# Twenty-seven fp32 products in two halves: norm factors, norm sums and cross attention's values

## The chip, the cores and the metric

The kernel runs on one core of one Trainium2 chip. The metric is the device time of one execution in microseconds; lower is better. Before the change the median of three runs was 877.38 us (877.32 to 877.93). TensorE (PE) does the products, ScalarE (ACT) and VectorE (DVE) the elementwise work, GpSimd (POOL) a few masks and sums, and SyncE (SP) issues the transfers of the weights.

## The reference

Two transformer blocks run one after the other on 256 tokens of width 1024, all in fp32. Cut to what matters here:

```
# first block
u = rms_norm(h, g_mix) @ w_in
ya = diff_attention(...)            # 4 heads; each head's output is normed: rms_norm(o, g_subln)
yb = stick_breaking_attention(...)  # 8 heads
h = h + concat(ya, yb) @ w_out
# cross attention, 4 heads of 256 columns, over 256 memory rows
q = rms_norm(h, g_cross) @ w_xq;  k, v = split(rms_norm(mem, g_mem) @ w_xkv)
h = h + (softmax(q k^T / 16) v) @ w_xo
h = h + square(relu(rms_norm(h, g_mlp) @ w_up)) @ w_down          # MLP, 4096 wide
h = rms_norm(h, g_final)
# second block
proj = _rmsnorm(h, norm1_g) @ w_in                                 # 6308 columns
y_a, y_b = _nsa_mixer(...), _dilated_mixer(...)
x = h + (sigmoid(g_ma) * (y_a @ w_o_a) + sigmoid(g_mb) * (y_b @ w_o_b)) @ w_out
x = x + square(relu(_rmsnorm(x, norm2_g) @ w_up)) @ w_down          # MLP, 4096 wide
# rms_norm(x, g) = x * rsqrt(mean(x*x) + 1e-6) * g
```

## The kernel before

Activations are kept with the model dimension on the partitions and the 256 tokens on the free axis, in eight chunks of 128x256.

**Split products.** Every weight matrix and every activation that meets one is split into a coarse part and a rest, both of type fp32r (`wunit`, lines 240 and 243, for weights; `split1` for activations). A product is then three products of one pass each: coarse by coarse, rest by coarse, coarse by rest. `mm3` (lines 276 to 278) does it with the weights stationary and 256 token columns streaming; `gemm_n` (lines 329 to 331) with the activations stationary and the weights' columns streaming, 256 or 292 of them; `acc_add` (lines 344 to 348) as `mm3` does, in another order. `gemm_t` and `out_rows` call `mm3`: the MLPs, the queries of cross attention, the memory's keys, the gates and all output matrices are of this kind. The projections of the mixers are mostly `gemm_n`.

**Full fp32 products.** Products of small tensors are not split; they stay fp32, and each leaves two records on PE. Transposes (line 449) leave one. Among the full products are:

- `row` (line 432): per-token factors, which stand one to a partition, are put on a diagonal, and a matrix of ones spreads them over all 128 rows: one product of 128x128 by 128x256. It is called five times: for the first block's norm, for the memory's norm, for cross attention's, and twice for the second block's.
- `rstd_t` (line 441): a matrix of ones sums squares over the partitions and spreads the sums, again one product by 256 columns. It is called for each of the four heads in `da_values`, and once in each MLP, after unit 2 of 16.
- `cross_values` (line 918): probabilities, transposed, by the memory's values. For each of four heads there are two halves of the output (`j`) and two halves of the memory (`kt`): four products by 256 columns, 16 in all. All go to one PSUM bank, which `split1` then reads.

Other full products keep their shape: the scores (lines 560 to 563, 660 to 663, 894), the stick-breaking sums (578 to 580), the values of the other attentions (670 to 673, 707, 708), and the sums of `rstd_n` (line 408), whose streamed operand has one column.

**Order.** `build` writes the blocks one after the other; inside a stage a `Filler` mixes generators of projection products into the attention heads' code. The order on each engine is then settled by a planner: the kernel is built under `tile.TileContext(nc, schedule_with_timeline_sim=True)`, which lays the program out by its own estimates, and by dependences that the code adds (`after`). `row` takes such a dependence for its product (`after`). All weight transfers go out on SP's queue into six raw buffers. The PSUM pool has three banks `G`, two `Z`, two `X` and one `O`; the results of the three changed functions all use `O`.

Of the kernel before, what the change touches and what calls it, by code (L numbers as in the profile page):

```python
# [17 lines left out]
P = 128  # L18
T = 256
NT = 2  # L20
# [114 lines left out]
class Builder:  # L135
# [289 lines left out]
    def row(self, r, tag, after=None):  # L425

        ps = self.Oo()
        d = self.t([P, NT, P], "diag")
        for tt in range(NT):
            self.nc.vector.tensor_scalar(out=d[:, tt], in0=self.ident, scalar1=r[:, tt:tt + 1], scalar2=None,  # L430
                                         op0=ALU.mult)
        i = self.nc.tensor.matmul(ps[:, :T], self.ones, d.rearrange("p t q -> p (t q)"), start=True, stop=True)
        if after is not None:
            self.after(i, after)
        out = self.t([P, T], tag)
        self.row_copy = self.nc.scalar.activation(out, ps[:, :T], AF.Copy)
        return out

    def rstd_t(self, acc, n, tag):
        ps = self.Oo()  # L440
        self.nc.tensor.matmul(ps[:, :T], self.ones, acc, start=True, stop=True)
        r = self.t([P, T], tag)
        self.rsqrt(r, ps[:, :T], 1.0 / n)
        return r
# [462 lines left out]
    def cross_values(self, p, mv, h, o):  # L907
        nc, mm = self.nc, self.nc.tensor.matmul
        ps = self.X((P, 2, T))
        for kt in range(NT):  # L910
            for tt in range(NT):
                self.transpose(ps[:, kt, tt * P:(tt + 1) * P], p[:, tt, kt * P:(kt + 1) * P])
        pt = self.t([P, 2, T], "xpt")
        nc.scalar.activation(pt, ps, AF.Copy)
        po = self.Oo((P, 2, T))
        for j in range(2):
            for kt in range(NT):
                mm(po[:, j], mv[:, kt, (2 * h + j) * P:(2 * h + j + 1) * P], pt[:, kt], start=(kt == 0), stop=(kt == 1))
        self.split1(o[0][:, 2 * h:2 * h + 2], o[1][:, 2 * h:2 * h + 2], po)


# [631 lines left out]
```

## Time and profile before

| | |
|---|---|
| median of 3 runs | 877.38 us (877.32 to 877.93) |
| profiled execution | 875.89 us, of which the span from the first to the last instruction is 874.2 us |
| mean granted clock of TensorE | 0.997 |
| PE busy | 858.7 us (98%), 7099 records |
| DVE, ACT, POOL busy | 599.6, 552.6, 90.0 us |
| DMA | 144.68 MB, 166 GB/s in the mean |

The profile is of one execution. "Busy" is the time in which an engine has at least one instruction under way; products overlap in PE, so a record's duration (some 280 ns for a split product) is longer than the distance from its start to that of the next one. In the timeline, a row is a start time, a duration, and how many equal instructions in a row it stands for; the distance between the starts of two rows, divided by the number of products that begin in it, is the time that each takes from PE. A stretch is a piece of the span, given in us from its start.

### The profile page before, as it was taken

How to read it: one execution, taken by the hardware profiler on the slowest of the kernel's cores; microseconds unless marked ns; L12 is line 12 of the kernel's file. 1: busy time of each engine (PE TensorE's matmuls, PEld its weight loads, DVE VectorE, ACT ScalarE, POOL GpSimd, SP SyncE). 2: the span in 40 equal slices, each digit the busy share in tenths (PEclk: the TensorE clock that was granted, in tenths of full speed). 3: DMA queues.
4: the chain of work that ended last, by engine and by line, in shares of the span. 5: the costliest groups of instructions: out<-in, count | busy, mean ns of one | idle time of the engine just before them, and what ended most of it. 6: DMA issues, size and time to landing. Idle time of an engine off the chain costs nothing.

```text
span 874.2 us, 18293 instructions
## 1 busy us (share of the span) xinstructions
PE 858.7 (98%) x7099; PEld 824.5 (94%) x7099; DVE 599.6 (69%) x1295; ACT 552.6 (63%) x1204; POOL 90.0 (10%) x131
## 2 busy tenths in 40 slices
PE   9999999999999999999999999999988999999998
PEld 9989989999999999999998998889977999999997
DVE  7646687585698555665977786786947985555564
ACT  7769577564565555664674987877755665555551
POOL 0032200020020000000203130113410300000000
PEclk9999999999999999999999999999999999999999
DMA  9664535652466566766377454232623565556531
GB/s 312 191 198 160 167 96 150 198 185 73 146 204 196 184 187 192 239 200 196 86 254 240 121 170 121 73 97 74 220 95 94 166 216 184 187 193 192 182 134 49
DMA packets 111862, 144.68 MB, mean 166 GB/s; under 512 B 6304, under 2 KB 100128, under 8 KB 111776
## 3 DMA queue, kind: packets, MB, share of 16 engines
q1 hardware_dynamic: 111216, 143.10, 52.4%
q8 instruction: 55, 0.90, 0.4%
q10 hardware_dynamic: 560, 0.42, 0.1%
q14 instruction: 31, 0.25, 0.1%
HBM read 142.46 MB, written 1.05 MB: 164 GB/s over the span
## 4 chain that ended last, share of the span: by engine, by line
PE 85%; DMA 5%; DVE 4%; ACT 3%; issue 1%; POOL 1%; SPq 0%; DVEq 0%; ACTq 0%; POOLq 0%
PE G L276 11%; PE G L277 11%; PE G L278 11%; PE Z L278 4%; PE Z L276 4%; PE Z L277 4%; PE G L331 4%; PE G L329 4%; PE G L330 4%; PE X L276 4%; PE X L278 4%; PE X L277 4%; PE X L449 3%; DMA wraw<-w_in 3%; PE Z L660 1%
## 5 line engine op out<-in xcount | busy, mean ns | idle before, releaser
L243 DVE TENSOR_TENSOR wlo<-wraw,whi 128x512 fp32r<-128x512 f32 (+2 forms) x513 | 347.9, 692 | 175.7 <-ACT whi L240 173.5
L240 ACT ACTIVATE whi<-wraw 128x512 fp32r<-128x512 f32 (+2 forms) x513 | 313.1, 623 | 197.3 <-PE G L278 86.0
L276 PE MATMUL G<-acth,whi 128*128 128x256 f32 x892 | 253.0, 285 | 1.8 <-ACT sbv L548 0.9
L277 PE MATMUL G<-acth,wlo 128*128 128x256 f32 x892 | 251.6, 283 | 0.0
L278 PE MATMUL G<-actl,whi 128*128 128x256 f32 x892 | 249.1, 283 | 0.0
L276 PEld LDWEIGHTS G<-acth,whi 128*128 128x128 f32 x892 | 169.4, 190 | 4.4 <-ACT sbv L548 1.1
L277 PEld LDWEIGHTS G<-acth,wlo 128*128 128x128 f32 x892 | 171.0, 192 | 0.6
L278 PEld LDWEIGHTS G<-actl,whi 128*128 128x128 f32 x892 | 168.0, 190 | 0.2
L329 PE MATMUL G<-whi,acth 128*128 128x256 f32 x400 | 113.8, 284 | 0.0
L331 PE MATMUL G<-whi,actl 128*128 128x256 f32 x400 | 113.6, 284 | 0.0
L330 PE MATMUL G<-wlo,acth 128*128 128x256 f32 x400 | 113.1, 283 | 0.0
L329 PEld LDWEIGHTS G<-whi,acth 128*128 128x128 f32 x400 | 75.2, 188 | 1.7 <-ACT whi L240 0.4
L331 PEld LDWEIGHTS G<-whi,actl 128*128 128x128 f32 x400 | 75.2, 188 | 1.0 <-issue 0.4
L330 PEld LDWEIGHTS G<-wlo,acth 128*128 128x128 f32 x400 | 75.0, 188 | 0.8 <-issue 0.4
L276 PE MATMUL X<-mhl,whi 128*128 128x256 f32 x240 | 67.5, 281 | 0.5 <-DVE mt L1505 0.5
L276 PE MATMUL Z<-mhl,whi 128*128 128x256 f32 x240 | 67.4, 281 | 0.0
L277 PE MATMUL Z<-mhl,wlo 128*128 128x256 f32 x240 | 67.4, 281 | 0.0
L278 PE MATMUL Z<-mhl,whi 128*128 128x256 f32 x240 | 67.4, 281 | 0.0
L277 PE MATMUL X<-mhl,wlo 128*128 128x256 f32 x240 | 67.4, 281 | 0.0
L278 PE MATMUL X<-mhl,whi 128*128 128x256 f32 x240 | 67.4, 281 | 0.0
L687 ACT ACTIVATE p<-p,mx 128x256 f32<-128x256 f32 x88 | 39.0, 445 | 11.4 <-DVE mx L680 7.4
L277 PEld LDWEIGHTS Z<-mhl,wlo 128*128 128x128 f32 x240 | 46.0, 192 | 0.0
(395 smaller groups left out, 1515.2 us busy)
## 6 DMA issues: line engine op xcount, KB each, us to landing
wraw<-w_up SPq DMA_DIRECT2D x64, 512.0 KB, 3.9
wraw<-w_down SPq DMA_DIRECT2D x64, 512.0 KB, 3.6
wraw<-w_in SPq DMA_DIRECT2D x42, 512.0 KB, 4.0
wraw<-w_dil SPq DMA_DIRECT2D x18, 512.0 KB, 4.0
wraw<-w_xkv SPq DMA_DIRECT2D x16, 512.0 KB, 3.4
wraw<-w_out SPq DMA_DIRECT2D x16, 512.0 KB, 3.9
wraw<-w_in SPq DMA_DIRECT2D x21, 256.0 KB, 5.6
wraw<-w_xq SPq DMA_DIRECT2D x8, 512.0 KB, 3.7
```

The costliest lines, as they stand in the source:

```text
L240: self.part_made = nc.scalar.activation(hi[:, rs], r[:, rs], AF.Copy)
L243: i = nc.vector.tensor_tensor(out=lo[:, rs], in0=r[:, rs], in1=hi[:, rs], op=ALU.subtract)
L276: mm(out, w[0], x[0], start=first, stop=False, skip_group_check=True)
L277: mm(out, w[1], x[0], start=False, stop=False, skip_group_check=True)
L278: self.last_mm = mm(out, w[0], x[1], start=False, stop=last, skip_group_check=True)
L329: mm(outs[tt], x[0][:, k, ts_], w[0], start=first, stop=False, skip_group_check=True)
L330: mm(outs[tt], x[0][:, k, ts_], w[1], start=False, stop=False, skip_group_check=True)
L331: mm(outs[tt], x[1][:, k, ts_], w[0], start=False, stop=(k == KC - 1), skip_group_check=True)
L449: self.mark = self.nc.tensor.transpose(out, in_, self.ident[:n, :n])
L660: i = mm(z[:, 0:256], q[rs, P:T], k[rs, 0:256], start=True, stop=True)
L687: self.nc.scalar.activation(s[:, sl], s[:, sl], AF.Exp, scale=-1.0, bias=m[:, i:i + 1], accum_out=sums[:, i:i + 1])
```

## The change

Each product of the three functions by 256 columns becomes two by 128 columns each, with the same stationary operand, into the two halves of the same PSUM region. The first of the products into a bank has `start`, the others add to or fill what it has cleared. The sums, the dependences that `row` takes, and the instructions that read the results are the same.

```diff
@@ def row
-        i = self.nc.tensor.matmul(ps[:, :T], self.ones, d.rearrange("p t q -> p (t q)"), start=True, stop=True)
-        if after is not None:
-            self.after(i, after)
+        for tt in range(NT):
+            i = self.nc.tensor.matmul(ps[:, tt * P:(tt + 1) * P], self.ones, d[:, tt], start=(tt == 0), stop=(tt == 1),
+                                      skip_group_check=True)
+            if after is not None:
+                self.after(i, after)
@@ def rstd_t
-        self.nc.tensor.matmul(ps[:, :T], self.ones, acc, start=True, stop=True)
+        for tt in range(NT):
+            self.nc.tensor.matmul(ps[:, tt * P:(tt + 1) * P], self.ones, acc[:, tt * P:(tt + 1) * P], start=(tt == 0),
+                                  stop=(tt == 1), skip_group_check=True)
@@ def cross_values
-                mm(po[:, j], mv[:, kt, (2 * h + j) * P:(2 * h + j + 1) * P], pt[:, kt], start=(kt == 0), stop=(kt == 1))
+                for tt in range(NT):
+                    c = slice(tt * P, (tt + 1) * P)
+                    mm(po[:, j, c], mv[:, kt, (2 * h + j) * P:(2 * h + j + 1) * P], pt[:, kt, c],
+                       start=(j == kt == tt == 0), stop=(kt == 1), skip_group_check=True)
```

## Rows read from the trace of the kernel before

**Rows 1.** The page: span, and busy time of each engine.

```profile
span 874.2 us, 18293 instructions
...
PE 858.7 (98%) x7099; PEld 824.5 (94%) x7099; DVE 599.6 (69%) x1295; ACT 552.6 (63%) x1204; POOL 90.0 (10%) x131
```

**Rows 2.** Waits of PE: us in total, times, longest.

```profile
PE X L449 <- ACT pt L702: 1.8, 1, 1.8
PE Z L344 <- ACT acth L296: 1.2, 1, 1.2
```

**Rows 3.** Lines 432, 441, 918: records, ns min/median/max, first and last start.

```profile
L432 PE MATMUL O<-diag,ones x10: 377/378/483, 24.0 to 673.6; 128*128 128x256 f32 x10
...
L441 PEld LDWEIGHTS O<-ss,ones x4: 187/188/188, 261.9 to 710.7; 128*128 128x128 f32 x4
...
L918 PE MATMUL O<-xpt,mv x32: 377/379/382, 206.8 to 224.3; 128*128 128x256 f32 x32
```

**Rows 4.** Timeline, 222 to 224 us: start, duration, line, count.

```profile
222.83 1.89 PE L918 MATMUL O<-xpt,mv 128*128 128x256 f32 x8
```

**Rows 5.** Timeline, passes of 128 columns (40 us) and of one (433 us).

```profile
40.65 0.38 PE L579 MATMUL Z<-p,nones 128*128 128x128 f32 x2
40.87 0.39 PE L580 MATMUL Z<-p,c_tri 128*128 128x128 f32 x2
...
433.04 1.03 PE L408 MATMUL O<-one,ss 128*128 128x1 f32 x8
```

**Rows 6.** Timeline of PE, 130 to 138 us.

```profile
130.42 0.28 PE L330 MATMUL G<-wlo,acth 128*128 128x256 f32 x1
...
132.12 0.28 PE L330 MATMUL G<-wlo,acth 128*128 128x256 f32 x1
...
132.46 0.59 PE L441 MATMUL O<-sq,ones 128*128 128x256 f32 x2
...
133.48 0.49 PE L449 MATMUL X<-c_ident,p 128*128 128x128 f32 x3
...
134.04 0.28 PE L331 MATMUL G<-whi,actl 128*128 128x256 f32 x1
...
135.40 0.28 PE L331 MATMUL G<-whi,actl 128*128 128x256 f32 x1
...
135.84 0.60 PE L708 MATMUL O<-pt,dav 128*128 128x256 f32 x2
...
136.40 0.28 PE L331 MATMUL G<-whi,actl 128*128 128x256 f32 x1
...
137.10 0.28 PE L331 MATMUL G<-whi,actl 128*128 128x256 f32 x1
```

**Rows 7.** Stretches: length, busy us (instructions), granted clock, DMA share, GB/s.

```profile
156.00:182.00 26.00, 26.00 (x232) 26.00 (x231) 17.27 (x26) 16.35 (x33) 4.89 (x5) 1.00 0.57 179
224.37:262.01 37.64, 37.64 (x320) 37.61 (x319) 29.65 (x45) 24.46 (x45) 6.82 (x7) 1.00 0.59 188
262.25:420.70 158.45, 158.45 (x1346) 158.42 (x1345) 102.86 (x188) 88.58 (x152) 0.00 (x0) 1.00 0.64 195
673.62:710.68 37.06, 37.06 (x316) 37.03 (x315) 33.68 (x56) 24.51 (x46) 6.77 (x7) 1.00 0.62 199
710.92:868.50 157.58, 157.58 (x1339) 157.55 (x1338) 93.15 (x141) 80.28 (x133) 0.00 (x0) 1.00 0.51 162
```

**Rows 8.** PE by line, 31.8 to 39 us: busy us, mean ns, idle.

```profile
L276 PE MATMUL G<-acth,whi 128*128 128x256 f32 x22 | 6.1, 276 | 0.0
```

**Rows 9.** The same, 94.6 to 98.5 us.

```profile
L276 PE MATMUL G<-acth,whi 128*128 128x256 f32 x12 | 3.3, 281 | 0.0
```

**Rows 10.** Timeline of PE, 710.5 to 714 us.

```profile
710.68 0.59 PE L441 MATMUL O<-ss,ones 128*128 128x256 f32 x2
...
711.46 0.28 PE L276 MATMUL G<-acth,whi 128*128 128x256 f32 x1
...
713.58 0.28 PE L276 MATMUL G<-acth,whi 128*128 128x256 f32 x1
```

## The prediction

> **What bounds the kernel now.** I read the page's first part, then PE's own waits, then the timeline of TensorE. PE is busy 858.7 of 874.2 us [rows 1], and the longest thing it ever waits for costs 1.2 to 1.8 us, once each [rows 2]. So the kernel lasts as long as its products, and the question of any change is what PE then does in each nanosecond. The granted clock is 1.00 in all long stretches [rows 7], which is the level of 2.4 GHz, so the clock gate has no part here.
>
> The timeline shows two things that the page hides. First, a full fp32 product leaves two records, that is two passes: line 432 has 10 records for 5 products, line 918 32 for 16 [rows 3], and line 441 12 for 6. Second, the products of split operands (lines 276 to 278, 329 to 331, 344 to 348; one pass of 256 columns each; the five stretches of [rows 7] hold little else, and half of PE's 7099 records [rows 1]) follow each other at one of **two spacings**. From 156 to 182 us 230 of them start in 26.00 us, 113 ns each (the row's count less the two that only reach into the stretch). From 262.25 to 420.70 us 1344 start in 158.45 us, 118 ns each, and the stretches from 224, 674 and 711 us give 118 too [rows 7]. At 711 us 18 products take 2.12 us, 117.8 ns each [rows 10]. The same line on the same tiles shows it in its mean duration as well: 276 ns in the one case, 281 in the other [rows 8, 9]. Data, clock and engine are the same in both, and PE is busy all the time in both, so neither waits nor bandwidth make the difference.
>
> What comes between two such runs decides which one follows. In one stretch of line 329 to 331 work the spacing is 113 ns (15 products in 1.70 us), then line 441 passes and it is 118; three transposes pass and it is 113 again (12 in 1.36 us); line 708, 256 columns wide, passes and it is 117 (6 in 0.70 us) [rows 6]. A run that is once at 113 ns stays there until the next product of another kind; a run at 118 sometimes finds 113 later. I went through the timeline and noted each run of six or more split products that begins on lines 276 to 278 at full clock, and the pass just ahead of it. Behind a pass of 128 columns (transposes of line 449, and lines 563, 580, 663) 21 of 27 runs are at 113 ns within their first ten products: line 563's at 31 us is the first of them [rows 8], line 580's at 94 us one of the six that are not [rows 9]. Behind a pass of 256 columns it is 3 of 11; line 441's at 711 us is the last of the eight at 118 [rows 10]. Runs that begin on lines 329 to 331 are at 118 in either case (at 113: 2 of 25, and none of 9 with one odd case, behind a stall, left out); the transposes in [rows 6] are one of the two.
>
> **The change, part by part.** 27 full products (5 of `row`, 6 of `rstd_t`, 16 of `cross_values`) become two of half the width.
>
> *Their own passes.* Eight passes of 256 columns take 1.89 us with the last one's 0.38 of latency: seven spacings in 1.51, 0.216 each, 0.431 per product [rows 4, 3]. Two passes of 128 columns follow each other at 0.11 us (line 579 at 40.65, line 580 at 40.87) [rows 5], and passes of a single column, which have nothing but their weight load, at 0.113 (seven in 1.03 less the 0.24 of the last) [rows 5]. So four half passes cost 0.44 to 0.45: 0.01 to 0.02 more each, 27 times 0.25 to 0.5 us. I take **+0.35**. Below nothing it can't go: the columns streamed are the same. From above, if a half pass could not begin before its own load (188 ns, [rows 3]) had ended, four would take 0.75 and the whole 8.7 us; rows 5 are nearer by far, as they have the same shape.
>
> *What they leave behind.* Behind four of these products lies a long run. Line 918 at 224 us: 318 split products; line 441 at 262 us: 1344 up to 420.7 (the next 10 us have a third spacing of 120, which I leave alone); line 432 at 674 us: 314; line 441 at 711 us: 1337 [rows 7]. All four begin on lines 276 to 278 and all four are at 118 today. Behind a half pass three in four of such runs were at 113. If all four turn, 3313 products at 4.5 ns less: **-14.8 us**. The first few of a run are still at 118: 4 times 6 at 4.5 ns, 0.1 us back. Line 441 at 147 us and line 432 at 441 us are followed by lines 329 to 331; I count nothing for them, nor for the short runs behind the others. The other bound is none: all stay at 118, as line 580's run at 94 us did, and 0 us come back.
>
> By the Trainium skill, page "TensorE: Matmul & The Clock Gate", section "Back-to-back issue gap", a warm product costs its columns at 2.4 GHz and a fixed 2.5 ns. For 256 columns that would be 109 ns with no second value, and the rows show 113 and 118; by it 54 more passes cost 0.14 us and nothing is gained.
>
> *Waits.* In `row` the first half needs only the first of two diagonal tiles, so it can start one VectorE instruction sooner; the end is still set by the second. The copy behind both halves is one instruction as before. In `cross_values` the split of the result waits for all eight halves; PE waits for one such split, 1.2 us ahead of line 344 [rows 2], and that stays. I price all of these at nothing, with the waits of [rows 2] as the most that can go.
>
> *Order.* The planner lays out a program with 27 more products, so pieces around 190 to 225 us can change places. Split products cost the same wherever they stand; what can change is a wait, and which short run is fast.
>
> *Sum.* -14.8 + 0.1 + 0.35 = -14.3. The profiled execution took 875.89 (its span 874.2), which gives 861.6; the median of the runs is 877.38, 1.5 above, and on that scale it is **863 us**.
>
> **Rivals.** *One MLP only.* The two runs of 1344 and 1337 have the same code, so I expect them to go together; if one stays at 118, 6.0 us are missing: 869, or 871 with one of the short ones at 118 as well. For: line 449's run at 607 us stayed at 118 for 153 products behind a half-width pass. Against: both are entered alike today.
>
> *No change of rate.* The spacing has another cause than the width ahead (the tiles, say), or two passes of ordinary fp32 don't act as transposes do: of the six cases at 118 one is line 580, the nearest in shape, with one run at each spacing. Then only +0.35 is left, 877.7, or 875 if the two short runs turn and the MLPs don't. The rule of the Trainium skill given above, which knows one spacing, comes out here as well.
>
> *Slower: the cross stage opens up.* Between 190 and 225 us each head's values are followed by ACT's and DVE's split of them, and today PE waits for one head's only, 1.2 us. If the planner puts the extra products where split products now cover the other three heads, three more such waits come in: 3.6 + 0.35, 881.3. It decides once more than 1.4 us of waits are added and no long run turns. Against it: PE has ready products of `w_xo` and `w_xq` all along there.
>
> *It doesn't do what it says.* If the records behind the change were still 256 columns wide, the time would be that of before; the slices in the code leave no room for it, and it gets no chance of its own.
>
> **How the numbers follow.** Both MLPs at 113 ns 0.56 (863 to 866, by the two short runs); one 0.12 (869 to 871); none 0.20 (875 to 877.9; in 0.03 of it enough of the short runs turn to be told from no change); slower by waits 0.12 (near 881). Two tenths of a per cent, 1.75 us, is about what can be told from no change. Faster: 0.56 + 0.12 + 0.03 = 0.71, same 0.17, slower 0.12. The range from 861.5 to 877.9 leaves out the slower case and a little below the forecast, under 2 in 10; the likeliest case's own is 862 to 867.
>
> **What would show it.** Lines 432, 441 and 918 with twice the records at 128 columns and 0.11 us apart; line 276 in the stretches behind 262 and 711 us with a mean of 276 instead of 281 ns, and 1344 products in 152.3 us instead of 158.4. If the mean stays 281 there, the central step is wrong. If the mean falls elsewhere, in stretches whose entry was not changed, the width is not the cause. If PE's waits in the cross stage grow by more than 1.4 us, the slower rival is at work.

## The result, and the profile after

The changed kernel takes **863.43 us** (median of 6 executions, 861.04 to 864.40) against 877.35 for the kernel before on the same chip (6, 873.79 to 877.93): a ratio of 0.987, 95% interval 0.984 to 0.990. The profiled execution took 863.68 us, 12.2 less than that of before.

The page of the changed kernel, against [rows 1]: PE has 54 records more and 12.7 us less to do, and is as busy as it was.

```profile
span 862.0 us, 18402 instructions
...
PE 846.0 (98%) x7153; PEld 813.1 (94%) x7153; DVE 599.7 (70%) x1295; ACT 552.7 (64%) x1204; POOL 91.1 (11%) x131
```

PE's longest waits are those of [rows 2], to the tenth (lines from the first edit on have moved down: 432, 441, 449, 702, 918 are now 433, 444, 453, 706, 924):

```profile
PE X L453 <- ACT pt L706: 1.8, 1, 1.8
PE Z L344 <- ACT acth L296: 1.2, 1, 1.2
```

The three changed lines, against [rows 3]: twice the records, 128 columns in each, 275 ns where it was 378.

```profile
L433 PE MATMUL O<-diag,ones x20: 270/275/377, 23.8 to 667.4; 128*128 128x128 f32 x20
...
L444 PE MATMUL O<-ss,ones x8: 270/274/275, 261.2 to 704.7; 128*128 128x128 f32 x8
...
L924 PE MATMUL O<-xpt,mv x64: 271/275/275, 205.8 to 223.6; 128*128 128x128 f32 x64
```

Four windows of the changed kernel, set to the four long runs of split products of [rows 7] (length, busy us and records of each engine, granted clock, DMA share, GB/s):

```profile
223.66:261.06 37.40, 37.40 (x320) 37.40 (x319) 29.51 (x45) 24.46 (x45) 6.82 (x7) 1.00 0.60 184
261.56:413.80 152.24, 152.24 (x1346) 152.24 (x1345) 102.21 (x187) 88.05 (x152) 0.00 (x0) 1.00 0.67 203
667.43:704.26 36.83, 36.83 (x315) 36.83 (x314) 33.38 (x56) 24.38 (x46) 6.77 (x7) 1.00 0.62 198
704.75:856.50 151.75, 151.75 (x1341) 151.70 (x1339) 93.22 (x141) 80.35 (x133) 0.00 (x0) 1.00 0.52 169
```

In the first MLP the row has 1346 records in 152.24 us, where [rows 7] has as many in 158.45. Without the two or three that only reach into the window, that is 113 ns a product in place of 118. In the second, 1341 records in 151.75 us give 113 again. The run behind cross attention's values (320 records, 37.40 us) and the one behind `row` at 667 us (315, 36.83) are at 117 to 118, as they were. The mean duration of line 276 says the same, as in [rows 8, 9]; by line, in 262 to 414 us and then in 224 to 261 us (busy us, mean ns, idle):

```profile
L276 PE MATMUL G<-acth,whi 128*128 128x256 f32 x207 | 57.1, 276 | 0.0
...
L276 PE MATMUL G<-acth,whi 128*128 128x256 f32 x48 | 13.3, 281 | 0.0
```

That is nearly the whole difference. The two MLPs from the sum to the end of their stage, in the kernel before (same columns):

```profile
262.25:430.97 168.72, 168.55 (x1429) 168.32 (x1428) 113.13 (x203) 97.81 (x172) 5.23 (x6) 1.00 0.61 187
710.92:874.20 163.28, 158.90 (x1346) 158.47 (x1344) 95.74 (x146) 80.28 (x133) 0.00 (x0) 1.00 0.51 162
```

The same two stretches of the changed kernel:

```profile
261.56:424.28 162.72, 162.47 (x1430) 162.26 (x1428) 112.69 (x203) 97.54 (x172) 5.21 (x6) 1.00 0.64 194
704.75:862.00 157.25, 152.86 (x1347) 152.47 (x1345) 95.61 (x146) 80.35 (x133) 0.00 (x0) 0.99 0.51 168
```

They give 6.00 and 6.03 us, 12.0 of the span's 12.2. What lies ahead of the first MLP became 0.7 us shorter, what lies between the two 0.5 us longer. In both stretches ScalarE, VectorE and the transfers do the same work in less time; what changed there is PE's pace.

### The profile page after: what moved, and what is told of

It reads as the page before. It is cut to its first block, busy times and chain, and to the rows that moved or that the text cites. A ratio compares the mean times of both kernels' runs of the same rounds, so it can differ in the third digit from the quotient of the medians.

```text
span 862.0 us, 18402 instructions
## 1 busy us (share of the span) xinstructions
PE 846.0 (98%) x7153; PEld 813.1 (94%) x7153; DVE 599.7 (70%) x1295; ACT 552.7 (64%) x1204; POOL 91.1 (11%) x131
## 4 chain that ended last, share of the span: by engine, by line
PE 91%; ACT 3%; DMA 2%; DVE 2%; issue 1%; POOL 0%; SPq 0%; ACTq 0%; POOLq 0%
PE G L276 12%; PE G L277 12%; PE G L278 12%; PE G L331 5%; PE G L329 5%; PE G L330 5%; PE Z L278 4%; PE Z L277 4%; PE Z L276 4%; PE X L276 4%; PE X L277 4%; PE X L278 4%; PE X L453 3%; DMA wraw<-w_in 2%; PE Z L664 2%; PE O L677 1%
## 5 line engine op out<-in xcount | busy, mean ns | idle before, releaser
L276 PE MATMUL G<-acth,whi 128*128 128x256 f32 x892 | 250.4, 282 | 1.9 <-ACT sbv L552 0.9
L277 PE MATMUL G<-acth,wlo 128*128 128x256 f32 x892 | 249.0, 280 | 0.3 <-DVE wlo L243 0.3
L278 PE MATMUL G<-actl,whi 128*128 128x256 f32 x892 | 245.7, 279 | 0.0
L277 PEld LDWEIGHTS G<-acth,wlo 128*128 128x128 f32 x892 | 168.4, 189 | 1.2 <-DVE wlo L243 0.5
L276 PE MATMUL X<-mhl,whi 128*128 128x256 f32 x240 | 66.4, 277 | 0.5 <-DVE mt L1512 0.5
L278 PE MATMUL X<-mhl,whi 128*128 128x256 f32 x240 | 66.3, 276 | 0.0
L276 PE MATMUL Z<-mhl,whi 128*128 128x256 f32 x240 | 66.3, 276 | 0.0
L278 PE MATMUL Z<-mhl,whi 128*128 128x256 f32 x240 | 66.3, 276 | 0.0
L276 PEld LDWEIGHTS X<-mhl,whi 128*128 128x128 f32 x240 | 45.1, 188 | 0.7 <-DVE mt L1512 0.7
```

What stands on the lines that cost most here:

```text
L276: mm(out, w[0], x[0], start=first, stop=False, skip_group_check=True)
L277: mm(out, w[1], x[0], start=False, stop=False, skip_group_check=True)
L278: self.last_mm = mm(out, w[0], x[1], start=False, stop=last, skip_group_check=True)
```

## The experiments

In the profiles I count the records in a fixed window inside each MLP (two or three of them only reach into it): 852 in 100 us is the 118 ns of the kernel before, 885 the 113 ns of the kernel after. Times are medians; the kernel before ran beside each set, with 876.05 us in the first, 875.38 in the second, 875.27 in the third and 875.43 in the last. In the code, `...` stands for what is left out, some lines are joined, and the comments are added here.

### Which of the 27 products it is

The MLPs' sums alone halved, all else as before:

```
-        self.nc.tensor.matmul(ps[:, :T], self.ones, acc, start=True, stop=True)
+        for c0, c1 in zip(cuts, cuts[1:]):
+            self.nc.tensor.matmul(ps[:, c0:c1], self.ones, acc[:, c0:c1], start=(c0 == 0), stop=(c1 == T), ...)
...
-                r = self.rstd_t(ss, D, "rb")
+                r = self.rstd_t(ss, D, "rb", (0, 128, 256))      # the heads keep (0, 256)
```

> Only the two products of rstd_t in the MLPs are halved; row, cross_values and the four heads keep 256 columns. Theory (the width of the pass just ahead sets the spacing of the run behind it): the runs behind both go to 113 ns, some 12.2 us below before (865.2), all of the change's gain. Rival (the gain is spread over the 27 products, or comes from the planner's new order in the cross stage): well under half of it, 871 or more.

And the complement, the kernel after with the MLPs' sums whole, cuts `(0, 256)`:

> The complement: row, cross_values and the heads' rstd_t are halved, the two products in the MLPs keep 256 columns. Theory: the MLPs stay at 118 ns (mean of line 276 there 281 ns), time within 1 us of before. Rival (spread over all, or planner's order): most of the 14 us are here.

Measured: 864.73 us for the first (4 executions, 861.53 to 867.06), a ratio of 0.987 (0.984 to 0.991); 876.21 for the second (10, 874.67 to 877.98), 1.001 (0.999 to 1.002). Windows in the MLPs of the first (length, PE's busy us and records, granted clock, DMA share, GB/s):

```profile
270.00:370.00 100.00, 100.00 (x885) 1.00 0.67 207
...
715.00:815.00 100.00, 100.00 (x885) 1.00 0.61 193
```

The same windows of the second:

```profile
270.00:370.00 100.00, 100.00 (x852) 1.00 0.65 199
...
715.00:815.00 100.00, 100.00 (x851) 1.00 0.58 187
```

Two of the 27 products carry the gain. The other 25 give nothing that can be told from zero.

### Is it the width of the pass just ahead

Two kernels, both made from the kernel before, give the MLPs products of both widths and differ in which comes last. Each adds one product into a part of the bank that nothing reads: 128 columns behind the whole sum (four passes in all), or 256 columns behind the halved one (six).

```
+        self.nc.tensor.matmul(ps[:, T:T + extra], self.ones, acc[:, 0:extra], start=False, stop=True, ...)
...
+                r = self.rstd_t(ss, D, "rb", (0, 256), 128)         # mlp_256_then_128
+                r = self.rstd_t(ss, D, "rb", (0, 128, 256), 256)    # mlp_128s_then_256
```

> In the MLPs the product of 256 columns stays whole, and a product of 128 columns that nobody reads is put behind it (6 passes' worth of work in place of 4 halves); the rest as before. Theory (the last pass counts): both MLPs at 113 ns, about 12 us below before. Rival (halving the whole product counts, e.g. by its end or by the missing wide passes): 118 ns, 877.7.

> In the MLPs the product is halved, and a product of 256 columns that nobody reads is put behind the halves; the rest as before. Theory (the last pass counts): both MLPs back at 118 ns, 877.7 to 878.3. Rival (any narrow pass in the group, or just more passes, sets it): 113 ns, 12 us below before.

Measured: 864.38 us (2 executions), ratio 0.987 (0.984 to 0.991), with a narrow pass last; 876.28 (8, 873.70 to 879.68), 1.000 (0.998 to 1.003), with a wide pass last. Windows in the MLPs of the first:

```profile
270.00:370.00 100.00, 100.00 (x885) 1.00 0.67 204
...
715.00:815.00 100.00, 100.00 (x885) 1.00 0.61 193
```

And of the second:

```profile
270.00:370.00 100.00, 100.00 (x851) 1.00 0.65 200
...
715.00:815.00 100.00, 100.00 (x851) 1.00 0.58 185
```

The first does more work than the kernel before and is 12 us faster. So neither the halving of the sum nor a saving in it makes the time; what stands ahead of the run does. That it is the width of the last pass is not shown by these two alone. The sums that worked have four passes, those that did not have two (whole) or six (this second kernel), and no kernel has four passes with a wide one last. A third one cuts the sum at column 64, cuts `(0, 64, 256)`, again four passes:

> The kernel before, with the MLPs' sum of squares alone as a product of 64 columns and then one of 192, in its own place. The theory that the last pass only has to be shorter than 256 columns: 113 ns behind it, some 864.7 us. The rival that a pass must be no longer than the 0.110 us of 128 columns: 118 ns, some 876 to 877 us. I lean to the first (0.55): 192 columns would end about 0.16 us after they start, nearer to the 0.11 of 128 than to the 0.2155 of 256 by a little only. The sum itself costs the same 512 columns in each kernel.

865.06 us (4 executions), 0.988 (0.986 to 0.991): 192 columns last do it as well. The theory that the last pass has to be as short as 0.110 us falls.

### Do the waits behind the pass matter

Behind the MLPs' sums the first split product waits for ScalarE's part of a new weight, the second for VectorE's. Behind the two runs that stayed at 118 ns nothing waits, which made the waits a rival. To take the waits away without touching a semaphore, the halved sum goes into the middle of a weight part:

```
-            run(self.gemm_t([self.wcols(w_up, 256 * u)], act, outs))
+            for k, _ in enumerate(self.gemm_t([self.wcols(w_up, 256 * u)], act, outs)):
+                if u == 3 and k == 2:
+                    r = self.rstd_t(ss, D, "rb", self.last_mm)      # pinned behind the last product,
+                    self.pin = self.sum_mm                          # the next one pinned behind it
```

> The kernel before, with the MLPs' sum of squares alone as two products of 128 columns, but issued in the middle of a weight part (between k = 2 and k = 3 of the fourth unit), so that the split products just behind them wait for nothing; in the earlier kernels the first two behind them wait, one for ScalarE, one for VectorE. Theory A, the width of the last pass alone decides in the MLPs: both long runs behind it lie at 113 ns a product and the time is near 864.7 us, as in the kernel with the halved sums in their own place. Theory B, a narrow pass turns a run only where the first two split products behind it each carry a wait: both runs stay at 118 ns and the time is near that of before, 876 to 877 us.

Median 865.03 us (5 executions), ratio 0.987 (0.984 to 0.990): the waits are not needed. But one of the five, the profiled one, took 873.94, and its windows show where most of it went:

```profile
270.00:370.00 100.00, 100.00 (x885) 1.00 0.67 208
...
715.00:815.00 100.00, 100.00 (x851) 1.00 0.58 187
```

The first MLP was at 113 ns, the second, behind the same code, at 118, which is 6 of the 9 us above the median. This execution also has the lowest granted clock of the five in the mean, 0.992 against 0.995 to 0.997. The other four took 863.3 to 865.4 us, too little for an MLP at 118. So, by the times, the same instructions get one spacing or the other from execution to execution.

### Can other runs be turned

If a narrow pass turned any run, the two long ones that stayed at 118 could be had as well. Two kernels add an unread 128-column product of the ones by the identity to each of the two output projections, `w_xo` and `w_out_2`, on top of the change:

```
+    def kick(self):
+        o = self.Oo()
+        self.pin = self.nc.tensor.matmul(o[:, :P], self.ones, self.ident, start=True, stop=True)
+        self.after(self.pin, self.last_mm)
...
+            if m == kick: self.kick()                                # kick_no_waits: mid-part
+                    if kick and j == 1 and ms[0] == 0: self.kick()   # kick_waits: ahead of a part
```

> The kernel after, with one more product of 128 columns of the ones by the identity, which nothing reads, inside two of the long runs that stayed at 118 ns behind a narrow pass: in that of cross attention's output projection and in that of the second block's output projection, at places where the split products behind it wait for nothing. Theory A, a narrow pass turns a run wherever it stands and it was chance that these two did not: at least one of the two runs turns to 113 ns behind it. Theory B, waits on the first two split products are needed: both stay at 118. Its time differs by under 1 us from the kernel after in either case, so it is read from the spacings.

> The kernel after, with the same unread product of 128 columns in the same two runs, but just ahead of a weight part whose first split product waits for ScalarE and whose second waits for VectorE, as behind the MLPs' sums (the second row of the last weight unit of each projection). Theory B: both runs turn to 113 ns from there on. Theory A without any role of waits: no more turns than in the kernel whose added products stand ahead of products without waits. If neither turns, something else than width and waits marks the MLPs' places. The time differs by under 1 us from the kernel after.

The first took 863.52 us, both projections at 118 ns behind the added products. The second took 871.15: `w_xo` stayed, `w_out_2` turned, and the second MLP was now at 118. Its windows in `w_out_2` and the second MLP (25 us hold 215 records in the kernel before):

```profile
675.00:700.00 25.00, 25.00 (x221) 1.00 0.61 196
715.00:815.00 100.00, 100.00 (x851) 1.00 0.59 190
```

Neither theory says that. A new one: the narrow sum met a run at 113 ns this time, and from 113 it leads to 118. The same kernel again, timed:

> The kernel with the unread 128-column products ahead of waiting weight parts in the two output projections once more, timed now: in its one execution the second projection's run turned to 113 behind the added product, the first projection's did not, and the second MLP's run, which the narrow sum met at 113 this time, lay at 118 (871.15 us). Theory C (what the narrow pass meets counts): so in all executions, near 871 us. The rival that a turn is a matter of chance in each execution: most executions near 863 to 865 us, some near 871.

Median 868.64 us (10 executions), 0.992 (0.988 to 0.995), and the ten split: 861.95 to 865.39 four times, 868.02 to 870.95 five times, 873.36 once. The profiled one again had `w_out_2` at 113 and the second MLP at 118. So neither is fixed: the added product shifts the odds of the second MLP, and by their times four executions escape (only two executions of this kernel were profiled, both at 118 there). A test of the new theory puts one more narrow product (two passes, where the sum has four) halfway through each MLP, where it meets a run at 113 ns:

```
+            if u in (9,): self.kick()
```

> The kernel after, with one more product of 128 columns of the ones by the identity, which nothing reads, halfway through each MLP (behind the tenth unit's down products, ahead of a weight part whose first split product waits for ScalarE and whose second waits for VectorE), so that a narrow pass meets a run which is already at 113 ns. Some 750 split products of the first MLP's run and 670 of the second's stand behind it. Theory C, the spacing ahead of the narrow pass counts, and from 113 it leads to 118 (as it did for all eight narrow passes met so far at 113 in the traces of these kernels): both halves behind it lie at 118, 1,420 x 4.45 ns = 6.3 us and 0.5 us for the two products, near 870 us. Theory D, at these places a narrow pass leads to 113 whatever was ahead: nothing but the 0.5 us, near 864 us. I take C at 0.6.

865.42 us (4 executions), 0.990 (0.985 to 0.994). Windows ahead of and behind the added product, in either MLP:

```profile
270.00:340.00 70.00, 70.00 (x620) 1.00 0.66 198
345.00:415.00 70.00, 70.00 (x621) 1.00 0.71 214
715.00:785.00 70.00, 70.00 (x620) 1.00 0.63 195
792.00:862.00 70.00, 69.60 (x615) 1.00 0.43 138
```

620 in 70 us is 113 ns, and it stays there (the last window reaches into the end of the kernel). As I had put it, for any narrow pass, theory C falls: a run at 113 is not spoilt by a single narrow product. For a sum of four passes it was not tested here. The profiled execution is also the slowest of the four, 868.63 us at a mean granted clock of 0.991 (862.41 us at 1.000 is the fastest), with both MLPs at 113. So a time near 868 alone does not show an MLP at 118; the five executions of 868.02 to 870.95 above had 0.996 to 0.999.

### From 118, halfway through an MLP

The same added product on the kernel before, whose MLPs are at 118 ns:

> The kernel before, its MLPs' sums whole, with the same unread product of 128 columns halfway through each MLP, so that it meets a run at 118 ns. If any narrow pass turns a run at 118 where the two split products behind it wait (C and D both say so), the halves behind it lie at 113 ns and the time is near 876 + 0.5 - 6.3 = 870 us; that the gain goes with the number of split products behind the pass would be shown with it. If only the place of the sums themselves does it, 876.5 us.

875.25 us (10 executions), 1.000 (0.997 to 1.004): no gain. In the profiled execution:

```profile
270.00:340.00 70.00, 70.00 (x597) 1.00 0.63 190
345.00:415.00 70.00, 70.00 (x597) 1.00 0.71 209
715.00:785.00 70.00, 70.00 (x620) 1.00 0.63 196
792.00:862.00 70.00, 70.00 (x620) 1.00 0.45 143
```

597 is 118 ns: the added product left the first MLP there. And the second MLP was at 113 from its beginning, behind a **whole** sum of 256 columns. So wide passes too leave 113 now and then; three of this kernel's ten executions (869.7 to 871.5 us) have the time of one MLP at 113, and so have two of the 19 of the kernel before, with nothing added, that ran beside it (869.20 and 869.92 us). An added product that did nothing and a halved sum that works differ in the number of passes, two against four (the order test's whole sum with a product of 128 behind it has four too, two of them narrow). So, two added products:

```
-        self.pin = self.nc.tensor.matmul(o[:, :P], self.ones, self.ident, start=True, stop=True)
+        for tt in range(NT):
+            self.pin = self.nc.tensor.matmul(o[:, tt * P:(tt + 1) * P], self.ones, self.ident, ...)
```

> The kernel before with two unread products of 128 columns, as many passes as the halved sums have, in place of the one halfway through each MLP, which left the first MLP's run at 118 ns. Theory E, the number of narrow passes ahead of the run counts (the halved sums are four passes, the added product was two): both halves behind them turn to 113 ns, 1,420 x 4.45 ns = 6.3 us less than before and 1.0 us more for the products, near 870 us in most executions. Theory F, the place counts and each execution draws its spacing there, whatever the number: 118 ns behind them and near 876 us in most executions, with some near 870. I take E at 0.5.

871.68 us (5 executions, 868.96 to 874.29), ratio 0.995 (0.992 to 0.998), so 4.6 us less (2.1 to 7.1) where 5.3 were expected of a full success:

```profile
270.00:340.00 70.00, 70.00 (x597) 1.00 0.63 191
345.00:415.00 70.00, 70.00 (x620) 1.00 0.72 216
715.00:785.00 70.00, 70.00 (x597) 1.00 0.61 188
792.00:862.00 70.00, 70.00 (x620) 1.00 0.47 149
```

Both MLPs go from 118 to 113 ns at the added products, with weights, activations, banks and waits alike on either side of them. It is the cleanest sight of the effect, and the gain goes with the number of products behind the pass: half the run, about half the gain. Four passes are not a rule by themselves, though: `row` at 667 us has four of them and leaves 118. But what it meets is a run at 113 ns already, here in the changed kernel (two of the 64 records only reach into the window):

```profile
660.00:667.00 7.00, 7.00 (x64) 1.00 0.51 156
```

Pace met and number of passes together sort the long runs of all profiles better than either alone (read from the starts of the products just ahead and behind). In the MLPs and at `row`, four passes, the last of 192 columns or fewer, left 113 in 17 of 18 cases where they met 118, and 118 in 8 of 8 where they met 113: `row` in six profiles, and the second MLP's sum in the two profiles whose `w_out_2` had turned. The added single products, two narrow passes, left the pace as it was in 8 of 10 (5 of 7 met at 118, 3 of 3 met at 113). So for four passes theory C fits after all. The sixteen narrow passes of `cross_values` met 118 and left 118 in 6 of 6. Whole products, 256 columns last, left 118 in 25 of 26, whichever pace they met. I found this order afterwards, and no run was made to test it. Two added products halfway through the MLPs of the changed kernel would do so: by it they would send the second halves back to 118.

## Why the prediction was right, and where it was not

863 us forecast, 863.43 measured, the likeliest case (both MLPs at 113 ns).

- **Their own passes, +0.35.** The shape is as forecast. In the timeline of the changed kernel nine spacings of line 924 take 1.28 us less the last pass's 0.275, 0.112 each:

```profile
221.96 1.28 PE L924 MATMUL O<-xpt,mv 128*128 128x128 f32 x10
```

  The 0.35 itself is below what a profile can show beside the 0.7 and 0.5 us by which the other stages moved, and the 25 products alone came out at +0.2 us, within their interval.
- **Four long runs, -14.8: half right.** The two MLPs turned and gave 12.0 us; the step takes 2681 of its 3313 products from them (12.1 us at its 4.5 ns). The two shorter runs, 632 products and 2.8 us, did **not** turn. The step rested on one count over short runs of many kinds ("Behind a half pass three in four of such runs"), and that count does not hold for a place. In the six profiles of kernels with halved `row` and `cross_values`, the 12 runs right behind them at 224 and 667 us were at 118 every time. The step took the width of the pass as the only condition. The pace of the run ahead and the number of passes count as well: `row` met 113 ns in all six profiles.
- **The cause, "the width ahead".** Shown is that the passes just ahead of the MLPs' runs make the difference. That their width does is only partly shown: in the MLPs' sums a narrow last pass always came with four passes, a wide one with two or six, and two narrow passes alone left the first MLP at 118. It is also odds, not a switch. Over the profiled executions, an MLP's run behind its sum began at 113 ns in 15 of 18 cases with 192 columns or fewer last, and in 1 of 10 with 256 last. That one case is the sign that the prediction had named against itself, a pace that falls behind an entry that was not changed. That the rival *one MLP only* was given 0.12 was fair: it is what some executions of two of these kernels with halved sums did.
- **Waits, 0; order, 0.** Right: the two waits of [rows 2] are unchanged.
- **The sum.** The profiled executions differ by 12.2 us where -14.3 was forecast: the 2.8 us of the short runs are missing, and 0.7 us came from elsewhere, which was not traced further. That 863 and 863.43 agree more closely is in part luck: the forecast was put on the median of the first three executions (877.38), and the later sets of the kernel before have medians of 875.3 to 876.1, from which the change is worth about 12 us.
- **The rivals.** *No change of rate* and *slower* fell with the first profile. The first has a lesson: for 25 of the 27 products it was right.

What stays open is what sets the spacing. Number of passes, their width and the pace that they meet all shift the odds; place was not held apart from them. Neither the waits behind the passes nor the spacing that they meet decides alone. No run here shows a quantity that tells beforehand which way an execution will go. No version was found that beats the changed kernel: the added products turned `w_out_2` in both profiles of one kernel, worth 1 us, and, by the times, cost the second MLP its 6 us in six executions of ten.

## What to carry to other kernels

Where PE has no idle time, look at the distance between the starts of equal products, stretch by stretch: two stretches of the same code at 118 and 113 ns are 4% apart while both read as 100% busy. If the pace is set at the entry of a long run, the product to work on is the small one just ahead of that run, not the 1344 in it; try its shape, note the pace of the run that it meets, and test the reading by an unread product put between the two. Before counting on such a gain elsewhere, see it in that very place, in more than one execution.

## What the runs showed of the hardware

- At one granted clock (1.00), the same instructions on the same tiles run at 113 or 118 ns for over 1300 products in a row, with PE busy throughout at either pace (152.24 of 152.24 us, 158.45 of 158.45).
- By the times, an execution can draw either pace with the same code: the kernel with two unread products in its output projections took 862 to 865 us in four executions and 868 to 873 in six; its two profiled ones, 871.15 and 869.54 us, have the second MLP at 118.
- Four passes ahead of a long run, the last of 192 columns or fewer, left 113 ns in 17 of 18 cases where they met 118, and 118 in 8 of 8 where they met 113.
- A kernel with more work in it (a whole sum and an unread product of 128 columns) is 12 us faster than the one without.
